# A two-layer decoder trunk on one core: the down projections take the operands in two halves over four open column tiles

## The chip, the core and the metric

The kernel runs on one core of a Trainium2 chip. Five engines work side by side on that core, each in the order of its own instruction stream, and wait for each other by semaphores: TensorE (PE in the profile) multiplies matrices into PSUM, VectorE (DVE) and ScalarE (ACT) work element by element and may read PSUM, GpSimd (POOL) works element by element in SBUF, and SyncE (SP) issues the transfers from and to the device's memory. The metric is the time of one execution in microseconds (us) of device time; lower is better.

## The reference

The reference is two decoder layers over 256 tokens of width 1024. Each layer ends in a feed-forward block, and the change lies in that block alone:

```python
def conv_ffn(x, norm_g, w_up, conv_w, conv_b, w_down):
    s_ = x.shape[1]
    u = rmsnorm(x, norm_g) @ w_up
    up = jnp.pad(u, ((0, 0), (CONV_W - 1, 0), (0, 0)))
    c = conv_b + up[:, 0:s_] * conv_w[0]
    for j in range(1, CONV_W):
        c = c + up[:, j:j + s_] * conv_w[j]
    val, gate = jnp.split(c, 2, axis=-1)
    return (jax.nn.silu(gate) * val) @ w_down
...
    for l in range(DEPTH):          # DEPTH = 2: an mLSTM layer, then an attention layer
        h = h + (mixer of layer l)(h)
        h = h + conv_ffn(h, f_norm[l], f_w_up[l], f_conv_w[l], f_conv_b[l], f_w_down[l])
```

`w_up` is 1024 by 5632 (value and gate halves of 2816), `w_down` is 2816 by 1024, all in float32.

## The kernel before

The residual stream is kept transposed, as eight tiles of 128 features by 256 tokens (`hT`). Every float32 operand is split exactly into a high and a low part, and a product is three passes of parts. One call of `one(k)` in `steps_w`, called a step here, is two matmuls into one PSUM tile: the low weights by the high operand (256 columns, line 245) and the high weights by both parts of the operand side by side (512 columns, line 241). For k = 0 the order of the two is the other way round.

**The feed-forward block.** The up projection has 22 pairs, value and gate of 128 features each, in two PSUM tiles per pair. `finish` takes a pair out of PSUM (`whole`, lines 281 and 282), runs the three-tap convolution (lines 326 and 329), the gate (line 336) and the product (line 338), and splits the result into the high part (line 339, on ACT) and the low part (line 340, on POOL) of one of the 22 operands `f0` to `f21` of the down projection.

**The down projection.** It has eight column tiles, n = 0 to 7, of 128 features; each sums 22 steps, one for each operand. `down(n, ks)` gives the steps of tile n for the operands in ks. In the kernel before they go in this order: tile 0 with operands 0 to 18, tile 1 with 0 to 10, tile 0 with 19 to 21, tile 1 with 11 to 21, then tiles 2 to 7 whole. After a tile's last step, `residual` adds it to `hT` (lines 289 and 291); in layer 0 `feed` then makes the next stage's two sets of operands (lines 180 and 181), in layer 1 the tile is written out (line 293).

`project_out`, which the two mixers use for their output projections, already takes its operands in two halves over four column tiles (`GROUP = 4`), with eight steps to a tile.

**Weights.** `w_down` is held in 16 units per layer, two for each column tile: unit 2n has operands 0 to 10 of tile n, unit 2n + 1 has 11 to 21. A unit is loaded by one transfer of 704 KB on the SP queue into one of three `raw` buffers, and split in two pieces by ACT (line 171, the high part) and DVE (line 172, the low part) into one of four `hi` and four `lo` buffers. A unit is made when its first step is emitted, so the order of the steps is the order of the units too.

**What sets the order.** PE runs in the order of the program text. DVE, ACT, POOL and SP run in an order that a scheduler fixes at build time. Sums of this kind lie in a pool of five PSUM tiles, `pacc`, used in turn.

Of the kernel before, what the change touches and what calls it, by code (L numbers as in the profile page):

```python
# [20 lines left out]
S = 256  # L21
KD = D // P
NT = S // P
FF = 2816
KF = FF // P
# [4 lines left out]
DH = 128  # L30
# [6 lines left out]
AHEAD = 2  # L37
GROUP = 4
WARM = 8
WHOLE = 6  # L40
PIECES = 2

# columns of the per-partition parameter array
C_KVNORM, C_BNORM, C_FNORM, C_HN = 0, 8, 16, 32
# [3 lines left out]
N_PAR = C_CB + L * 2 * KF  # L48
# columns of the array that is needed first: the gates' weights, the first gain
C_WG, C_ANORM = 0, KD * 2 * MH  # L50
# [5 lines left out]
class Once:  # L56
    """A thing that is made when it is first asked for."""

# [9 lines left out]
def mix(steps, items=()):  # L68
    """Emit the steps, each a (cost, function), and the items, each a (time, function), among them."""
    items, now = list(items), 0.0  # L70
    for cost, step in steps:
        while items and items[0][0] <= now:
            items.pop(0)[1]()
        step()
        now += cost
    for _, item in items:
        item()
# [3 lines left out]
def yoco_kernel(ctx: ExitStack, tc: tile.TileContext, A, out):  # L81
    nc = tc.nc
    # the tensor engine works in the order of this program
    ctx.enter_context(tc.manual_schedule(engines={mybir.EngineType.PE}))
# [8 lines left out]

    # ---- the residual stream, transposed: hT[:, k] holds features k*128.. by tokens
    hT = keep.tile([P, KD, S], F32, name="hT")
    fst = const.tile([P, N_FIRST], F32, name="fst")
    par = const.tile([P, N_PAR], F32, name="par")
    # rows on every partition: the gates' biases, the gains of k's and q's first 32 features
    row = const.tile([P, N_ROW], F32, name="row")
# [17 lines left out]

    # the gates' weights: for each k the high parts, the low parts, and zeros
    wgs = wsp.tile([P, 2048], F32R, name="hi")[:, :KD * P]
    mhalf = const.tile([P, 8], F32, name="mhalf")  # L120
    nc.gpsimd.memset(mhalf, -0.5)
    # while the first loads run: the tensor engine's clock rises, the activation tables are loaded
    nc.scalar.activation(const.tile([P, 1], F32, name="tables"), mhalf[:, :1], AF.Exp)
    warm = const.tile([P, 512], BF16, name="warm")
    nc.vector.memset(warm, 0.0)
    for j in range(WARM):
# [3 lines left out]

    # ---- constants made on the chip
    ident = const.tile([P, P], F32, name="ident")
    make_identity(nc, ident)
    # adds rows m and m + 8
    both8 = const.tile([4 * MH, 2 * MH], F32, name="both8")
    nc.gpsimd.tensor_tensor(out=both8, in0=ident[:4 * MH, :2 * MH], in1=ident[:4 * MH, 2 * MH:4 * MH], op=OP.add)
    # sel[:, h] has ones in row h alone
    sel = const.tile([MH, MH, P], F32, name="sel")
    nc.gpsimd.memset(sel, 0.0)
    nc.gpsimd.affine_select(out=sel, in_=sel, pattern=[[-1, MH], [0, P]],  # L140
                            compare_op=OP.not_equal, fill=1.0, base=0, channel_multiplier=1)
    # [s, t], 1 where s <= t, else 0; columns 128.. are ones
    tri = const.tile([P, S], F32, name="tri")
    nc.gpsimd.memset(tri, 1.0)
    nc.gpsimd.affine_select(out=tri[:, :P], in_=tri[:, :P], pattern=[[1, P]],
                            compare_op=OP.is_ge, fill=0.0, base=0, channel_multiplier=-1)
    # mLSTM: [s, t], 0 where s <= t, else BIG; columns 128.. are free
    cmask = const.tile([P, S], F32, name="cmask")
# [4 lines left out]
    nc.gpsimd.tensor_copy(identb, ident)  # L153
    # attention: [t, s], columns 128.. 0 where s <= t, else -BIG; the columns before are free
    amaskf = const.tile([P, S], F32, name="amaskf")
# [5 lines left out]

    # ---- weights: a unit is loaded whole and split exactly into two float32r parts
    def unit(src, length, raw=None, pieces=PIECES):
# [18 lines left out]

    # ---- RMSNorm: the gain goes into the matmul's operand, 1/rms is applied to its result
    # an operand: for each k its high part, its low part, and both side by side
    def operand(pool, name, n):
# [20 lines left out]
    class Rstd:  # L206
        """1/rms of the residual stream: a column over the tokens and a row on every partition."""

# [15 lines left out]

    # ---- matmuls: three exact passes of hi and lo parts
    def steps_w(ps, w, at, x, ks, kall, done=None, apart=True):
        """ps[n, tokens] += W[k, n].T x[k, tokens]; at(k) gives the columns of k in w. The high parts of W
        times the low parts of x may be summed apart, in the second half of ps."""
        xh, xl, both = x
# [23 lines left out]
    def steps_x(t, units, x, done):  # L253
        """ps[tokens, 512] = x[k, tokens].T W[k, 512] over two units of four k."""
        xh, xl, _ = x
# [14 lines left out]
    def block_x(src, first, x, done):  # L270
        """Both token tiles of 512 columns: units first and first + 1 of src."""
        u = [Once(lambda j=j: unit(src[first + j], 2048)) for j in range(2)]
        return [s for t in range(NT) for s in steps_x(t, u, x, done)]
# [4 lines left out]
    def whole(ps, rows=P):  # L278
        """Both halves of a result of steps_w, in SBUF."""
        y = work.tile([P, S], F32, name="whole", bufs=WHOLE)[:rows]  # L280
        nc.scalar.activation(y, ps[:rows, S:], AF.Copy)  # L281
        nc.vector.tensor_tensor(y, ps[:rows, :S], y, OP.add)  # L282
        return y
# [13 lines left out]
    def project_out(src, x, gains, items):  # L297
        """GROUP columns' tiles go on with each operand as it comes, the items among their first half."""
        w = [Once(lambda u=u: unit(src[u], 2048)) for u in range(4)]
# [10 lines left out]

    # ---- ConvFFN
    def conv_ffn(l, gains):
        r = Rstd()
        with tc.tile_pool(name=f"ffn{l}", bufs=1, reuse_waits="tile") as fp, \
# [27 lines left out]
            def rescale():  # L342
                # the operands once more, with 1/rms in them
                r.row()
# [14 lines left out]
            ps = [[Once(acc) for half in range(2)] for i in range(KF)]  # L359
            # the first pairs go on with each operand as it comes  # L360
            mix([s for k in range(KD) for i in range(AHEAD) for s in pair_k(pair, i, k)],
# [15 lines left out]

            mix(down(0, range(19)) + down(1, range(11)) + down(0, range(19, KF)) + down(1, range(11, KF)))
            for n in range(2, KD):
                mix(down(n, range(KF)))  # L380
# [3 lines left out]

    # ---- layer 0: the first operands
    wgv = wgs.rearrange("p (k m) -> p k m", k=KD)
# [12 lines left out]
    with tc.tile_pool(name="mls", bufs=1, reuse_waits="tile") as mp, \  # L399
            tc.tile_pool(name="mlw", bufs=2, reuse_waits="tile") as mw:  # L400
        r = Rstd()
        # gates: parts of the input gates, then of the forget gates, by tokens
        psg = acc()
# [60 lines left out]
        def decay(h):  # L464
            # transposed: E[s, t] = exp(a_s - M_t), 0 where s > t
            mb = mis()[:, :S]
# [8 lines left out]

        # k and q by head, features by tokens
        kq = [mp.tile([P, S], F32, name=f"kq{j}") for j in range(2 * MH)]
# [15 lines left out]

        # the gates and the first unit go on with each operand as it comes
        def gate_step(k):
# [11 lines left out]

        # S^T times the decay weights
        PT = [[mp.tile([P, 384], F32R, name=f"PT{h}{j}") for j in range(2)] for h in range(MH)]
# [10 lines left out]

        # v with a column of ones and one of zeros: high parts, low parts
        V = [[mp.tile([P, MH, MV + 2], F32R, name=f"V{t}{j}") for j in range(2)] for t in range(NT)]
# [13 lines left out]

        # numerators and denominators, tokens by features
        hs = {}
# [24 lines left out]

        # output gates
        def o_done(nb):
# [18 lines left out]
        def at(t0, dt, fn, args):  # L584
            return [(t0 + dt * i, lambda a=a: fn(*a)) for i, a in enumerate(args)]
# [9 lines left out]

    # the rotation's tables with the gains of k and q in them; the other features' gains as columns
    tab = const.tile([P, 2, NT, 2, ROT], F32, name="tab")
# [13 lines left out]

    # ---- layer 1: attention over one block of 256 tokens
    with tc.tile_pool(name="att", bufs=1, reuse_waits="tile") as mp, \
# [4 lines left out]
        ys = {}  # L618
        # a query's factors: DH^-0.5 / rms, by head
        cq = mp.tile([P, NT, 2, 4], F32, name="cq")  # L620
        ncq = mp.tile([P, NT, 2, 4], F32, name="ncq")

        def heads(i, nb):
            def done(t, ps):
# [14 lines left out]
                if i == 0:  # L639
                    c = factor()  # L640
                    nc.vector.tensor_tensor(y, y, c[:, :, None].to_broadcast([P, 4, DH]), OP.mult)
                # rotate the first 32 features of each head
                r1 = mw.tile([P, 4, 2, HALF], F32, name="r1")
# [83 lines left out]
def _cols(w):  # L727
    """[k, n] -> units of 256 columns: [unit, 128, 8 * 256]."""
    k, n = w.shape
    return w.reshape(k // P, P, n // 256, 256).transpose(2, 1, 0, 3).reshape(n // 256, P, -1)  # L730


def _rows(w):
    """[k, n] -> units of 512 rows by 512 columns: [column block * 2 + row half, 128, 4 * 512]."""
    k, n = w.shape
    return w.reshape(2, 4, P, n // 512, 512).transpose(3, 0, 2, 1, 4).reshape(n // 256, P, 2048)
# [57 lines left out]
```

## Time and profile before

| | us |
|---|---|
| median of 3 runs | 608.62 (608.0 to 608.84) |
| span of the profiled execution, first to last instruction | 607.1 |
| PE busy | 593.5 (98% of the span) |
| DVE busy | 495.6 (82%) |
| ACT busy | 393.2 (65%) |
| POOL busy | 171.8 (28%) |

For the profiled execution the profile gives the span alone. A run's time also holds what lies ahead of the first and behind the last instruction; the median of the runs is 1.5 us above this span. Busy PE is modelled from the starts of its matmuls, so small gaps between matmuls count as busy.

### The profile page before, as it was taken

The numbers are of one execution on the slowest core, as the hardware profiler recorded it, in microseconds if no ns is written. First come the engines' busy times: TensorE is split into PE (matmuls) and PEld (weight loads), VectorE is DVE, ScalarE is ACT, GpSimd is POOL, SyncE is SP. The second block draws the span as 40 slices with busy tenths as digits, with TensorE's granted clock in tenths as the row PEclk, the third lists the DMA queues.
The fourth block names the chain that finished last, engine by engine and source line by source line (L and its number), as shares of the span: only waits on it lengthen the run. The fifth ranks groups of instructions, "written<-read, shape, count | busy, mean of one in ns | idle before, by whom it ended". The sixth has DMA issues, their size and how long they took to land.

```text
span 607.1 us, 8990 instructions
## 1 busy us (share of the span) xinstructions
PE 593.5 (98%) x3278; PEld 505.9 (83%) x3278; DVE 495.6 (82%) x837; ACT 393.2 (65%) x713; POOL 171.8 (28%) x186
## 2 busy tenths in 40 slices
PE   7899999999999999899999999999999999998997
PEld 4787888888888888788888878888888888887887
DVE  7897667989999999967768786467999999998550
ACT  5756776667886777755556687554878767675330
POOL 6600310352545344211111100022445453441000
PEclk8999999999999999899999999999999999999999
DMA  6874333526444543465754533335353445336530
GB/s 243 317 264 169 139 138 140 208 84 263 159 179 166 191 165 133 161 207 184 266 203 181 198 123 143 125 135 208 132 215 140 185 172 198 138 131 229 212 108 18
DMA packets 18621, 105.79 MB, mean 174 GB/s; under 512 B 2320, under 2 KB 3856, under 8 KB 9104
## 3 DMA queue, kind: packets, MB, share of 16 engines
q1 hardware_dynamic: 18576, 105.21, 47.0%
q8 instruction: 26, 0.43, 0.3%
q14 instruction: 19, 0.16, 0.1%
HBM read 104.15 MB, written 1.05 MB: 173 GB/s over the span
## 4 chain that ended last, share of the span: by engine, by line
PE 48%; DVE 37%; issue 8%; ACT 3%; POOL 2%; DMA 1%; SPq 0%; POOLq 0%; DVEq 0%; ACTq 0%
PE acc L241 15%; DVE y L329 15%; DVE lo L172 14%; PE acc L245 8%; PE acc L262 6%; PE acc L264 6%; PE acc L263 6%; DVE whole L282 4%; DVE xs L348 1%; ACT y L326 1%; DVE xa L181 1%; PE acc L239 1%; ACT hi L171 1%; DMA hT<-xT 1%; PE mis L547 1%
## 5 line engine op out<-in xcount | busy, mean ns | idle before, releaser
L172 DVE TENSOR_TENSOR lo<-raw,hi 128x1024 fp32r<-128x1024 f32 (+2 forms) x218 | 248.6, 1168 | 30.5 <-ACT hi L171 30.2
L241 PE MATMUL acc<-xb,hi 128*128 128x512 f32 x736 | 252.3, 396 | 0.6 <-POOL xb L351 0.6
L171 ACT ACTIVATE hi<-raw 128x1024 fp32r<-128x1024 f32 (+2 forms) x218 | 199.9, 964 | 61.3 <-PE acc L241 29.5
L245 PE MATMUL acc<-xb,lo 128*128 128x256 f32 x736 | 191.2, 279 | 0.0
L241 PEld LDWEIGHTS acc<-xb,hi 128*128 128x128 f32 x736 | 131.8, 188 | 26.3 <-POOL xb L351 1.3
L245 PEld LDWEIGHTS acc<-xb,lo 128*128 128x128 f32 x736 | 138.7, 188 | 8.0
L241 PE MATMUL acc<-f,hi 128*128 128x512 f32 x330 | 116.6, 398 | 1.0 <-POOL f L340 1.0
L329 DVE SCALAR_TENSOR_TENSOR y<-whole,par,y 128x254 f32<-128x254 f32 (+1 forms) x176 | 110.0, 644 | 3.2 <-ACT y L326 2.8
L245 PE MATMUL acc<-f,lo 128*128 128x256 f32 x352 | 97.5, 284 | 3.0 <-ACT f L339 3.0
L338 POOL TENSOR_TENSOR a<-sg,y 128x256 f32<-128x256 f32 x44 | 57.8, 1314 | 98.4 <-ACT sg L336 98.4
L241 PEld LDWEIGHTS acc<-f,hi 128*128 128x128 f32 x330 | 61.8, 190 | 14.5 <-POOL f L340 1.4
L245 PEld LDWEIGHTS acc<-f,lo 128*128 128x128 f32 x352 | 66.8, 190 | 5.0 <-ACT f L339 3.6
L326 ACT ACTIVATE y<-whole,par 128x256 f32<-128x256 f32 x88 | 51.7, 594 | 20.8 <-DVE whole L282 18.8
L241 PE MATMUL acc<-xa,hi 128*128 128x512 f32 x160 | 57.5, 401 | 0.7 <-DVE hT L291 0.5
L262 PE MATMUL acc<-hi,xa 128*128 128x512 f32 x128 | 53.4, 417 | 0.0
L340 POOL TENSOR_TENSOR f<-a,f 128x256 fp32r<-128x256 f32 x44 | 42.3, 962 | 36.6 <-ACT f L339 36.6
L264 PE MATMUL acc<-hi,xa 128*128 128x512 f32 x128 | 50.1, 391 | 0.0
L199 POOL TENSOR_TENSOR sqacc<-sqacc,sq 128x256 f32<-128x256 f32 x18 | 16.3, 908 | 119.0 <-ACT sq L198 119.0
L263 PE MATMUL acc<-lo,xa 128*128 128x512 f32 x128 | 50.0, 391 | 0.0
L245 PE MATMUL acc<-xa,lo 128*128 128x256 f32 x160 | 44.4, 289 | 0.8 <-DVE lo L172 0.7
L282 DVE TENSOR_TENSOR whole<-acc,whole 128x256 f32<-128x256 f32 (+1 forms) x97 | 39.4, 412 | 0.0
L281 ACT ACTIVATE whole<-acc 128x256 f32<-128x256 f32 (+1 forms) x97 | 35.4, 368 | 6.0 <-PE acc L241 5.8
(180 smaller groups left out, 637.7 us busy)
## 6 DMA issues: line engine op xcount, KB each, us to landing
raw<-w_up SPq DMA_DIRECT2D x44, 1024.0 KB, 4.8
raw<-w_down SPq DMA_DIRECT2D x32, 704.0 KB, 4.0
raw<-w_kqv SPq DMA_DIRECT2D x12, 1024.0 KB, 4.8
raw<-w_vo SPq DMA_DIRECT2D x8, 1024.0 KB, 4.8
raw<-w_out SPq DMA_DIRECT2D x4, 1024.0 KB, 4.8
raw<-w_o SPq DMA_DIRECT2D x4, 1024.0 KB, 4.8
raw<-w_kq SPq DMA_DIRECT2D x2, 1024.0 KB, 7.8
raw<-w_kq SPq DMA_DIRECT2D x4, 256.0 KB, 5.5
```

The costliest lines, as they stand in the source:

```text
L171: nc.scalar.activation(hi[:, c], raw[:, c], AF.Copy)
L172: nc.vector.tensor_tensor(lo[:, c], raw[:, c], hi[:, c].bitcast(F32), OP.subtract)
L241: nc.tensor.matmul(p, hi[:, c], both[k], start=k == 0, stop=last)
L245: nc.tensor.matmul(p[:, :S], lo[:, c], xh[k], start=False, stop=False)
L262: nc.tensor.matmul(p, xh[k][:, ts], hi[:, c], start=k == 0, stop=False)
L263: nc.tensor.matmul(p, xh[k][:, ts], lo[:, c], start=False, stop=False)
L264: nc.tensor.matmul(p, xl[k][:, ts], hi[:, c], start=False, stop=k == KD - 1)
L282: nc.vector.tensor_tensor(y, ps[:rows, :S], y, OP.add)
L326: nc.scalar.activation(y, u, AF.Identity, bias=b, scale=w[2])
L329: nc.vector.scalar_tensor_tensor(y[:, d:], u[:, :S - d], w[j], y[:, d:], op0=OP.mult, op1=OP.add)
L338: nc.gpsimd.tensor_tensor(out=a, in0=sg, in1=y[0], op=OP.mult)
L340: nc.gpsimd.tensor_tensor(out=al[i], in0=a, in1=ah[i].bitcast(F32), op=OP.subtract)
```

## The change

A constant `HOLD = 4` is new, and the last lines of `conv_ffn` emit the steps in another order. Comments are taken out elsewhere, and all lines below the constant move down by one, so that line 241 of before is line 242 after. The number of matmuls, weight units, transfers and vector operations is the same.

```diff
+HOLD = 4
...
-            mix(down(0, range(19)) + down(1, range(11)) + down(0, range(19, KF)) + down(1, range(11, KF)))
-            for n in range(2, KD):
+            for ks in (range(KF // 2), range(KF // 2, KF)):
+                for n in range(HOLD):
+                    mix(down(n, ks))
+            for n in range(HOLD, KD):
                 mix(down(n, range(KF)))
```

On PE, layer 0, where tile 0 (`acc_2683`) meets the last operands, 30 steps after the projection's first, the kernel before has these rows (a name is the PSUM tile, then the operand and the part of the weights, each with its buffer's number; `f18_1257` is operand 18):

```order
L241 MATMUL acc_2738<-f10_1249,hi_2732 128x512
L245 MATMUL acc_2683<-f19_1258,lo_2709 128x256
L241 MATMUL acc_2683<-f19_1258,hi_2708 128x512
L245 MATMUL acc_2683<-f20_1259,lo_2709 128x256
L241 MATMUL acc_2683<-f20_1259,hi_2708 128x512
L245 MATMUL acc_2683<-f21_1260,lo_2709 128x256
L241 MATMUL acc_2683<-f21_1260,hi_2708 128x512
L245 MATMUL acc_2738<-f11_1250,lo_2777 128x256
```

Tile 0 returns for operands 19 to 21 right after the first half of tile 1 (`acc_2738`). In the changed kernel the same place, the end of tile 0, stands 22 steps later on PE, and these rows are the change to the second half and the end:

```order
L242 MATMUL acc_2776<-f10_1249,hi_2770 128x512
L246 MATMUL acc_2683<-f11_1250,lo_2802 128x256
L242 MATMUL acc_2683<-f11_1250,hi_2801 128x512
...
L246 MATMUL acc_2683<-f21_1260,lo_2802 128x256
L242 MATMUL acc_2683<-f21_1260,hi_2801 128x512
L246 MATMUL acc_2714<-f11_1250,lo_2839 128x256
```

Four tiles (`acc_2683`, `acc_2714`, `acc_2745`, `acc_2776`) have taken operands 0 to 10 before any takes operand 11, so operand 11 is first read after 44 steps and operand 21 after 54.

On DVE, layer 0, behind the convolution of the last pair (`y`), the kernel before has these rows (`lo` is the low part of a weight unit, `hT` with `acc` the residual's sum):

```order
L172 TENSOR_TENSOR lo_2777<-raw_2774,hi_2776 128x704 x2
L329 SCALAR_TENSOR_TENSOR y_2665<-whole_2662,par_80,y_2665 128x255
L329 SCALAR_TENSOR_TENSOR y_2665<-whole_2662,par_80,y_2665 128x254
L172 TENSOR_TENSOR lo_2816<-raw_2813,hi_2815 128x704 x2
L172 TENSOR_TENSOR lo_2847<-raw_2844,hi_2846 128x704
L289 TENSOR_TENSOR hT_78<-acc_2683,hT_78 128x256
L172 TENSOR_TENSOR lo_2847<-raw_2844,hi_2846 128x704
L291 TENSOR_TENSOR hT_78<-acc_2683,hT_78 128x256
```

In the changed kernel the same stretch of DVE reads:

```order
L173 TENSOR_TENSOR lo_2771<-raw_2768,hi_2770 128x704 x2
L330 SCALAR_TENSOR_TENSOR y_2665<-whole_2662,par_80,y_2665 128x255
L330 SCALAR_TENSOR_TENSOR y_2665<-whole_2662,par_80,y_2665 128x254
L173 TENSOR_TENSOR lo_2802<-raw_2799,hi_2801 128x704 x2
L173 TENSOR_TENSOR lo_2839<-raw_2836,hi_2838 128x704 x2
L173 TENSOR_TENSOR lo_2878<-raw_2875,hi_2877 128x704 x2
L173 TENSOR_TENSOR lo_2917<-raw_2914,hi_2916 128x704 x2
L290 TENSOR_TENSOR hT_78<-acc_2683,hT_78 128x256
L292 TENSOR_TENSOR hT_78<-acc_2683,hT_78 128x256
```

Up to the last `y` the kinds of rows are the same in both, and only which unit a split belongs to differs. Behind it, four whole units are split ahead of the first residual sum, where it was one and a half. Layer 1 differs in the same way. On SP, eleven loads of `w_down` in layer 1 stand ahead of the first output, where it was nine; POOL's order is the same in both.

## Rows read from the trace of the kernel before

**Rows 1.** The page, its 40 slices: the clock that TensorE was granted, in tenths.

```profile
PEclk8999999999999999899999999999999999999999
```

**Rows 2.** Busy us by stretch: PE, PEld, DVE, ACT, POOL; granted clock; DMA share; GB/s.

```profile
250.00:260.00 10.00, 8.19 (x38) 6.67 (x36) 8.78 (x13) 5.99 (x11) 1.75 (x3) 0.83 0.65 224
260.00:270.00 10.00, 10.00 (x59) 8.77 (x58) 6.76 (x12) 5.98 (x11) 0.86 (x1) 1.00 0.58 206
...
550.00:560.00 10.00, 7.83 (x44) 6.45 (x43) 8.81 (x13) 5.15 (x8) 1.61 (x2) 1.00 0.84 288
```

**Rows 3.** Who waited for whom, PE, 200 to 320 us: total, times, longest.

```profile
PE acc L245 <- ACT f L339: 1.3, 1, 1.3
PE acc L241 <- POOL f L340: 0.5, 1, 0.5
```

**Rows 4.** The same view of PE, 490 us to the end.

```profile
PE acc L245 <- ACT f L339: 1.7, 1, 1.7
...
```

**Rows 5.** Timeline of PE, layer 0: start, duration, what, idle before in brackets.

```profile
251.65 0.39 PE L241 MATMUL acc<-f,hi 128*128 128x512 f32 x1
...
252.00 0.39 PE L241 MATMUL acc<-f,hi 128*128 128x512 f32 x1
253.70 0.39 PE L245 MATMUL acc<-f,lo 128*128 128x256 f32 x1 [1.31 <-ACT f L339]
254.59 0.80 PE L241 MATMUL acc<-f,hi 128*128 128x512 f32 x1 [0.50 <-POOL f L340]
...
257.91 0.40 PE L241 MATMUL acc<-f,hi 128*128 128x512 f32 x1
```

**Rows 6.** Timeline of PE, layer 1.

```profile
550.04 0.39 PE L241 MATMUL acc<-f,hi 128*128 128x512 f32 x1
...
552.98 0.50 PE L241 MATMUL acc<-f,hi 128*128 128x512 f32 x1 [0.51 <-POOL f L340]
...
553.78 0.40 PE L241 MATMUL acc<-f,hi 128*128 128x512 f32 x1
```

**Rows 7.** Two equal stretches behind layer 0's wait, columns as in rows 2.

```profile
255.00:257.90 2.90, 2.90 (x10) 2.41 (x10) 2.76 (x6) 2.36 (x6) 0.00 (x0) 0.51 0.81 270
257.90:260.80 2.90, 2.90 (x19) 2.56 (x18) 1.84 (x4) 0.70 (x3) 0.00 (x0) 1.00 0.88 303
```

**Rows 8.** The matmuls of one tile name, by window: duration min/median/max, first and last start.

```profile
L241 PE MATMUL acc<-f,hi x32: 387/394/400, 241.0 to 252.0; 128*128 128x512 f32 x32
...
L241 PE MATMUL acc<-f,hi x32: 387/395/400, 539.1 to 550.0; 128*128 128x512 f32 x32
```

**Rows 9.** Timeline of DVE, layer 0.

```profile
243.42 2.22 DVE L172 TENSOR_TENSOR lo<-raw,hi 128x704 fp32r<-128x704 f32 x2
...
248.34 0.41 DVE L282 TENSOR_TENSOR whole<-acc,whole 128x256 f32<-128x256 f32 x1
248.68 2.22 DVE L172 TENSOR_TENSOR lo<-raw,hi 128x704 fp32r<-128x704 f32 x2
250.82 0.99 DVE L329 SCALAR_TENSOR_TENSOR y<-whole,par,y 128x255 f32<-128x255 f32 x2
251.73 2.22 DVE L172 TENSOR_TENSOR lo<-raw,hi 128x704 fp32r<-128x704 f32 x2
```

**Rows 10.** The instructions on one tile name: duration min/median/max in ns, first, last.

```profile
L289 DVE TENSOR_TENSOR hT<-acc,hT x32: 409/425/425, 101.0 to 603.8; 128x256 f32<-128x256 f32 x32
...
L181 DVE SCALAR_TENSOR_TENSOR xa<-hT,par,xa x24: 469/478/960, 102.7 to 419.4; 128x256 fp32r<-128x256 f32 x24
```

**Rows 11.** The page, transfers: count, KB each, us from issue to landing.

```profile
raw<-w_down SPq DMA_DIRECT2D x32, 704.0 KB, 4.0
```

**Rows 12.** Busy us in the attention's output projection (w_o), columns as in rows 2.

```profile
390.00:412.00 22.00, 22.00 (x136) 19.53 (x136) 16.10 (x27) 13.01 (x23) 3.57 (x4) 1.00 0.48 175
```

## The prediction

> **What bounds the kernel now.** I read the page's slices first, then the stretches of the two down projections, then PE's waits and its timeline there. The slices show TensorE at its full clock everywhere but at the start and in the 17th slice [rows 1], which lies in layer 0's down projection. By stretches, PE is busy 8.19 of 10 us at 250 to 260, with a mean granted clock of 0.83, and 7.83 of 10 at 550 to 560 in layer 1, at full clock; ten us later in layer 0 it is at 10.00 of 10 [rows 2]. So PE bounds both projections, but for a hole in each. The list of PE's waits says what the holes are: in 120 us around layer 0's projection there are two entries, both for an `f` operand of that projection, its high part from ACT (line 339) and its low part from POOL (line 340) [rows 3], and in layer 1 the same two [rows 4, 6]. The timeline gives the place: PE takes operand 20 at 252.00, waits for operand 21 until 254.59, and then goes slowly until 257.91 [rows 5]. DVE explains why operand 21 is late: the convolution of the last pair, at 250.82, stands behind a weight unit's split at 248.68, and the next split follows it at 251.73 [rows 9].
>
> **The change, step by step.** It removes no work. It moves operand 21's first use from step 32 of the projection (19 + 11 steps, then operands 19, 20, 21) to step 54 (four tiles with 11 steps each, then operands 11 to 21).
>
> *What the holes cost.* Steps start every 0.35 us (251.65 and 252.00 [rows 5]). From 252.00 to 257.91 PE makes six steps, which at that pace take 2.10 us and took 5.91: 3.81 us lost. Of it, 2.24 us is the wait (254.59 - 252.00 - 0.35), and 1.57 us is the slow stretch behind it (five steps in 3.32 us, against 1.75). That the slow stretch is the clock is seen in two equal stretches of 2.9 us: 10 matmuls at a granted 0.51, then 19 at 1.00 [rows 7], so the lower of the two levels, 1.2 GHz, came after a wait of 2 us with one matmul in it. In layer 1 there are three steps from 550.04 to 553.78 [rows 6]: 3.74 - 1.05 = 2.69 us lost, all of it wait, since the clock stays at 1.00 [rows 2]. Together 6.50 us.
>
> *Does operand 21 come in time after?* The projection's first step is at 241.0 [rows 8], so step s starts at about 241.0 + 0.35 s. Operand 21 is complete when PE goes on at 254.59 [rows 5] and is wanted at 241.0 + 54 x 0.35 = 259.9: 5.3 us early. In layer 1 the projection starts at 539.1 [rows 8], and the operand is there at 552.98 [rows 6] for a step at 558.0: 5.0 us early. DVE's order up to the last `y` is the same as before, so the operand is made no later than it was.
>
> *Do the weights come in time?* Units are used in the order 0, 2, 4, 6, 1, 3, 5, 7, each for 11 steps (3.85 us), so the same number per microsecond as before. The third is split on DVE by 245.6 (243.42 + 2.22) and wanted at step 22, 248.7. The fourth is split from 248.68 to 250.9 [rows 9]; its first half, there at about 249.8, is wanted at step 33, 252.6: 2.8 us early. The fifth (251.73 [rows 9], first half at about 252.8) is wanted at step 44, 256.4: 3.6 us early. Layer 1 has the tightest of them: its projection starts 298.1 us after layer 0's [rows 8] and the unit comes in the same rhythm, so I take 2 us as the least margin. From the fifth on DVE goes through four units without the residual's sums between them, 8.9 us by 2.22 each, and PE uses a unit in 3.85 us, so the splits stay ahead. The four `hi` and `lo` buffers help: a unit is now given back every 3.85 us, while before, unit 1 was held from step 11 to the end of the wait.
>
> *Do the PSUM tiles come in time?* Four held tiles and the next one are all five of `pacc`. Each takes the place of a pair's tile, in the order in which the pairs are taken out. The last of these reads is at 248.34 to 248.75 [rows 9], and its place goes to tile 4, wanted at step 88, 271.8. Tile 3, wanted at 252.6, takes the place before it, which was read earlier still.
>
> *What moves behind.* Tile 0 is done at step 55 instead of 33, tile 1 at 66 instead of 44, tile 2 at 77 instead of 66, tile 3 at 88 as before. So the first four residual sums come every 3.85 us. Each brings DVE two sums and two operand parts in layer 0, 2 x 0.43 + 2 x 0.48 [rows 10], besides a unit's split: 4.0 us with the 2.22 of rows 9, a little over 3.85. Three such rounds leave DVE about half a microsecond late, and the weights are units ahead by then. Tiles 4 to 7 are as before, and DVE was busy 6.76 of 10 us there [rows 2]. On SP, loads and outputs change places in layer 1: the 12th load of `w_down` waits for the first output, due at 539.1 + 55 x 0.35 = 558.4 and some 0.9 us of sums; with 4.0 us to land [rows 11] and 2.2 to split it is there by 566, for step 121, 581.5. All this I cost at nothing.
>
> *Sum.* 607.1 - 6.5 = 600.6 us of span. The runs' median is 1.5 us above the span profiled, which gives 602.1. The loss in the profiled execution need not be the median run's: the clock fell behind one of two like waits, so a run before may have had none, one or two such falls, at 1.57 each. If the median run had two, the time outside the span is nearly nothing and the changed kernel is at 608.62 - 8.07 = 600.5; if it had none, at 608.62 - 4.93 = 603.7.
>
> **The rivals.**
>
> *The clock falls elsewhere.* The waits go, but one stretch at the lower level turns up in the projection or a later stage: 602.1 + 1.6 = 603.7. For it: the two waits were alike, and one brought a fall and one none, so what starts one is not read from the wait's length alone. Against it: apart from the start and behind that wait, no slice has less than 9 tenths [rows 1], and no other wait of PE is in these stretches [rows 3, 4].
>
> *Another wait takes the place.* PE stops at tile 3 for the fourth unit, the tightest of the margins above. That needs DVE to be over 2 us later than in rows 9, and then costs what is beyond 2 us; DVE's order and its inputs up to there are those of before. If half of the old wait came back in each layer, with no slow stretch: 602.1 + 2.4 = 604.5.
>
> *Nothing is gained.* If DVE, and not PE, set the pace through the projections, taking PE's hole away would only let PE wait at the next unit: 608.6. Against it: behind 260 DVE is busy 6.76 of 10 us and PE 10.00 [rows 2].
>
> *Slower.* Changing the PSUM tile might leave TensorE idle for moments, and each such moment might drop the clock. The change makes seven changes of tile among the held four where there were three, in two layers eight more. At 1.57 us for each fall: 602.1 + 8 x 1.57 = 614.7, and five falls are enough to eat the gain (6.5 / 1.57 = 4.1). Against it: the output projection of the attention steps through four held tiles in the same way, and has 22.00 of 22.00 us busy at a clock of 1.00 [rows 12]. The Trainium skill (TensorE: Matmul & The Clock Gate, A second HAM failure mode: psum-queue depth-cycling) describes this: a kernel that cycles through PSUM banks lets the engine idle briefly and often between groups of matmuls, and its clock swings between the two levels. By that rule the time would be this rival's; the stretch at 390 to 412 does not show it.
>
> **How the numbers follow.** A change within 0.2%, 1.2 us, can't be told from none here. The forecast, both waits gone and nothing in their place, has 0.80. The clock falling elsewhere has 0.08, part of the wait coming back 0.06, nothing gained 0.03, slower by the clock 0.03. The first three lie below 607.4, so faster has 0.94, same 0.03, slower 0.03. The range goes from the lower bound of the time outside the span, less the few tenths by which runs differ (600.5 - 0.3), to its upper bound with one fall of the clock (603.7 + 1.6): 600.2 to 605.3.
>
> **What the new profile would show.** PE's waits for `f` from lines 340 and 341 are gone from both projections; the slices are at 9 throughout behind the start; the stretch 250 to 260 has PE at 10.00 and the clock at 1.00. The first residual sum of layer 0's projection is near 260.5 instead of 255.4, and everything behind layer 0 is 3.8 us earlier, the end 6.5. I am wrong if PE waits for `lo` at the start of tile 2 or 3, if the clock is below 1 in either projection, or if PE waits at the start of the attention for operands that the bunched sums delay.

## The result, and the profile after

The changed kernel takes 602.35 us (602.21 to 602.65, 4 runs) against 608.73 us (608.0 to 610.46, 4 runs) of the kernel before on the same chip: a ratio of 0.9891, 95% interval 0.9875 to 0.9906. That is 6.4 us less, where 602.1 us, 6.5 us less, was forecast.

The page of the changed kernel gives this span, and this clock over the 40 slices. Against [rows 1] the 8 in the 17th slice is gone:

```profile
span 600.5 us, 8992 instructions
...
PEclk8999999999999999999999999999999999999999
```

Busy time by stretch of the changed kernel, columns as in [rows 2]; the two stretches that held the holes are full and at full clock, and DVE's busier time has moved to 260 to 270, where the first residual sums now come together:

```profile
250.00:260.00 10.00, 10.00 (x59) 8.78 (x58) 7.89 (x11) 6.05 (x10) 1.62 (x2) 1.00 0.70 216
260.00:270.00 10.00, 10.00 (x58) 8.74 (x58) 9.05 (x17) 7.17 (x14) 0.86 (x1) 1.00 0.76 257
...
550.00:560.00 10.00, 10.00 (x59) 8.79 (x58) 7.26 (x12) 4.99 (x7) 0.00 (x0) 1.00 0.89 279
```

The list of PE's waits, from 200 to 320 us and from 490 us to the end, has no entry at all, where [rows 3] and [rows 4] had the two for `f`. Why it is empty is seen on GpSimd and on TensorE. First GpSimd's last row for operand 21 in layer 0, then PE's last row for operand 20 and its first for operand 21, then where the attention's first projection begins:

```profile
253.53 0.82 POOL L341 TENSOR_TENSOR f<-a,f 128x256 fp32r<-128x256 f32 x1 [0.53 <-ACT f L340]
```

```profile
259.48 0.40 PE L242 MATMUL acc<-f,hi 128*128 128x512 f32 x1
259.71 0.28 PE L246 MATMUL acc<-f,lo 128*128 128x256 f32 x1
...
302.54 0.39 PE L263 MATMUL acc<-hi,xa 128*128 128x512 f32 x1
```

The operand is complete at 253.53 + 0.82 = 254.35, within 0.25 us of where it was before [rows 5], and PE reads it at 259.71, 5.4 us later. The attention begins 3.9 us earlier than in the kernel before, whose row is this; so much of the saving is made by then:

```profile
306.47 0.40 PE L262 MATMUL acc<-hi,xa 128*128 128x512 f32 x1
```

DVE of the changed kernel from the fourth unit's split to the first residual sum, to set beside [rows 9]:

```profile
248.46 2.23 DVE L173 TENSOR_TENSOR lo<-raw,hi 128x704 fp32r<-128x704 f32 x2
250.62 0.99 DVE L330 SCALAR_TENSOR_TENSOR y<-whole,par,y 128x255 f32<-128x255 f32 x2
251.53 2.23 DVE L173 TENSOR_TENSOR lo<-raw,hi 128x704 fp32r<-128x704 f32 x2
254.17 3.33 DVE L173 TENSOR_TENSOR lo<-raw,hi 128x704 fp32r<-128x704 f32 x4 [0.42 <-ACT hi L172]
259.16 1.69 DVE L173 TENSOR_TENSOR lo<-raw,hi 128x704 fp32r<-128x704 f32 x2 [1.65 <-ACT hi L172]
260.77 0.42 DVE L290 TENSOR_TENSOR hT<-acc,hT 128x256 f32<-128x256 f32 x1
```

Up to 253.76 DVE does what it did before, at the same pace. Then it splits three units with idle time between them, and the eighth unit is ready at 260.85 for a step at 240.8 + 77 x 0.35 = 267.8. The fourth unit was the tightest, as forecast: its first half was split by about 249.6 (248.46 and half of 2.23), for step 33 at 240.8 + 33 x 0.35 = 252.4, 2.8 us early. In layer 1 the same unit's split starts at 542.81, so its first half was there at about 543.9 for a step at 546.8, 2.8 us early as well.

### The profile page after: what moved, and what is told of

Same layout as the page of the kernel before. It is cut to its first block, busy times and chain, and to the rows that moved or that the text cites. A ratio compares the mean times of both kernels' runs of the same rounds, so it can differ in the third digit from the quotient of the medians.

```text
span 600.5 us, 8992 instructions
## 1 busy us (share of the span) xinstructions
PE 591.0 (98%) x3278; PEld 504.8 (84%) x3278; DVE 495.4 (82%) x837; ACT 393.0 (65%) x713; POOL 172.7 (29%) x186
## 4 chain that ended last, share of the span: by engine, by line
PE 87%; DVE 6%; ACT 3%; POOL 2%; issue 1%; DMA 1%; SPq 0%; DVEq 0%; POOLq 0%
PE acc L242 41%; PE acc L246 21%; PE acc L263 6%; PE acc L265 6%; PE acc L264 6%; DVE lo L173 3%; ACT hi L172 1%; DVE xs L349 1%; DVE xa L182 1%; PE acc L240 1%; DMA hT<-xT 1%; PE mis L551 1%; POOL tab L611 1%; DVE hT L292 1%; PE mis L666 1%
## 5 line engine op out<-in xcount | busy, mean ns | idle before, releaser
L242 PE MATMUL acc<-f,hi 128*128 128x512 f32 x330 | 115.0, 394 | 0.0
## 6 DMA issues: line engine op xcount, KB each, us to landing
raw<-w_kq SPq DMA_DIRECT2D x4, 256.0 KB, 5.4
```

Source lines behind the costliest of these rows:

```text
L242: nc.tensor.matmul(p, hi[:, c], both[k], start=k == 0, stop=last)
```

## The experiments

Nine kernels were run, in three sets, each beside the kernel before on its chip (608.84 to 608.97 us in the median). Each is the changed kernel with one edit, but for one that has operand 21 late in the old order: there the last lines of `conv_ffn` are those of before as well.

**Two tiles held, in halves.** Operand 21 falls back to step 32, and every weight unit is still used in one piece:

```diff
-HOLD = 4
+HOLD = 2
```

> Two tiles are held open instead of four, again in halves of eleven operands. Operand 21 is then first wanted at step 32 (11 + 11 + 10), the same step as in the kernel before, while every weight unit is used in one piece, as in the changed kernel. My theory (what counts is the step at which operand 21 is first wanted): both waits are back, 608.6 us, 608.0 to 610.5. Rival (the gain is from the units, each given back after 11 steps, or from the plain halves): 602.4, as with four.

Measured: 609.04 us (607.87 to 611.6), ratio 1.0004 (0.9989 to 1.0019). The whole gain is gone. PE's waits in layer 0:

```profile
PE acc L246 <- ACT f L340: 1.8, 1, 1.8
PE acc L242 <- POOL f L341: 0.5, 1, 0.5
```

The same two waits of [rows 3] are back in both layers, so neither the halves nor the units' order gain anything by themselves while operand 21 is wanted at step 32.

**Three tiles held.** Operand 21 is wanted at step 43:

```diff
-HOLD = 4
+HOLD = 3
```

> Three tiles are held open. Operand 21 is wanted at step 43: 241.0 + 43 x 0.35 = 256.1 in layer 0, and it is there at 254.5; 539.1 + 15.1 = 554.2 in layer 1, there at 553.0. My theory: both waits are gone with 1.2 to 1.6 us to spare, and the time is that of four tiles, 602.4 (602.0 to 603.0). Rival (four open tiles are needed, the gain goes by the number of tiles): between the two kernels, 604 to 607.

Measured: 602.4 us (602.29 to 603.17), ratio 0.9892 (0.9869 to 0.9914), as with four. In its trace operand 21 is complete at 254.44 and the projection starts at 240.9, so step 43 is at 256.0: 1.5 us to spare are as good as 5.4.

**Two tiles held, nineteen operands each.** Operand 21 is wanted at step 40:

```diff
-            for ks in (range(KF // 2), range(KF // 2, KF)):
-                for n in range(HOLD):
+            for ks in (range(19), range(19, KF)):
+                for n in range(2):
                     mix(down(n, ks))
-            for n in range(HOLD, KD):
+            for n in range(2, KD):
```

> Only two tiles are held, but each takes 19 operands before it stops: tile 0 with 0 to 18, tile 1 with 0 to 18, then 19 to 21 of either. Operand 21 is wanted at step 40, 255.0 in layer 0 (there at 254.5) and 553.1 in layer 1 (there at 553.0). My theory: the waits are gone or a few tenths of a us each, 602.4 to 603.0. Rival (halves, or more than two open tiles, are what gains): 607 to 609.

Measured: 602.31 us in the median (602.27 to 606.58), ratio 0.9887 (0.9862 to 0.9913); the run of 606.58, the profiled one, has some ten us at the lower clock between 20 and 35 us, before either projection. This is one of these stretches; the changed kernel has 30 matmuls there at a clock of 1.00:

```profile
25.00:30.00 5.00, 5.00 (x18) 4.15 (x17) 3.19 (x7) 0.97 (x3) 0.00 (x0) 0.50 0.46 187
```

PE has no wait in either projection here. Operand 21 is complete at 258.86 for a step at 245.3 + 40 x 0.35 = 259.3 in layer 0 (all of it later by the slow stretch), and at 553.11 for 553.5 in layer 1: 0.4 us to spare were enough. Two tiles suffice when they keep PE busy until step 40. With two tiles in halves, which end in the waits, this says that the step of operand 21 counts, not the number of tiles.

**One layer at a time.** For layer 0 (and the same with 1):

```diff
+            if l == 0:
+                for ks in (range(KF // 2), range(KF // 2, KF)):
+                    for n in range(HOLD):
+                        mix(down(n, ks))
+            else:
+                mix(down(0, range(19)) + down(1, range(11)) + down(0, range(19, KF)) + down(1, range(11, KF)))
+                for n in range(2, HOLD):
+                    mix(down(n, range(KF)))
             for n in range(HOLD, KD):
```

> The new order in layer 0 alone, the old one in layer 1. My theory: the two waits are independent; layer 1's stays, at 2.7 us, 602.4 + 2.7 = 605.1, or 606.6 if the clock falls behind it in this run. Rival (nearly all the gain is in one layer, or a saving in layer 0 only lets layer 1 wait longer): 602.4 or 608.7.

> The new order in layer 1 alone, the old one in layer 0. My theory: layer 0's wait stays, at 2.2 us without and 3.8 us with the slow stretch behind it: 604.6 to 606.2. Rival: 602.4 or 608.7, as for layer 0 alone. The two gains, 608.7 less this time and 608.7 less that of layer 0 alone, should add up to the 6.4 us of the whole change within 1.6, one fall of the clock.

Measured: 604.66 us for layer 0 alone (604.55 to 604.94), ratio 0.9928 (0.9906 to 0.995); 606.46 us for layer 1 alone, ratio 0.9953 (0.9937 to 0.997). The second is 0.3 us above the range expected. Against the 608.92 us of before in this set that is 4.26 us and 2.46 us, together 6.7, where both give 6.4 to 6.6. So the two holes are independent, to within 0.3 us. Of the ten runs of layer 1 alone two are at 604.65 and 604.76, six from 606.02 to 606.78 and two near 607.5. The profiled run is the one of 604.76, and in its trace layer 0's wait is there and the clock does not fall behind it, while in [rows 2] the same wait has 0.83:

```profile
250.00:260.00 10.00, 8.17 (x46) 6.72 (x45) 9.20 (x15) 7.00 (x13) 1.72 (x3) 1.00 0.71 226
```

So the wait itself costs 604.7 - 602.35 = 2.35 us. The six runs above it by 1.3 to 2.1 us fit a slow stretch like the 1.57 us of [rows 5], but only the run of 604.76 has a trace, so where they lost it is not shown.

**Tiles in turn.** Tiles 4 and 5 step by step:

```diff
-            for n in range(HOLD, KD):
+            mix([s for k in range(KF) for n in (4, 5) for s in down(n, [k])])
+            for n in range(6, KD):
                 mix(down(n, range(KF)))
```

> The changed kernel, with tiles 4 and 5 of both layers taken in turn, one step of each: 43 changes of the PSUM tile per layer where there was one. My theory: a change of tile costs TensorE nothing, 602.4 (602.0 to 603.5), and the granted clock stays at 1.00 in that stretch. Rival (changes of tile leave idle moments and bring the clock down): 1.6 us for each fall, and a clock below 1 around 272 to 288 us; five falls make it 610.

Measured: 602.36 us (602.31 to 603.17), ratio 0.9888 (0.9867 to 0.991). The stretch with the 43 changes, as busy time, and three matmuls in it, the last of one step and the two of the next, which goes into the other tile:

```profile
272.00:288.00 16.00, 16.00 (x94) 14.00 (x92) 8.02 (x14) 6.22 (x11) 0.79 (x1) 1.00 0.53 183
```

```profile
273.03 0.39 PE L242 MATMUL acc<-f,hi 128*128 128x512 f32 x1
273.26 0.28 PE L246 MATMUL acc<-f,lo 128*128 128x256 f32 x1
273.38 0.40 PE L242 MATMUL acc<-f,hi 128*128 128x512 f32 x1
```

Steps start 0.35 us apart as within one tile, and the clock stays at 1.00. The rival that ended slower is refuted for tiles whose operands are there.

**Operand 21 made late.** Multiplications by one on GpSimd, in place, behind the last pair's product; four of them in the new order, four in the old order, eight in the new:

```diff
                 nc.gpsimd.tensor_tensor(out=a, in0=sg, in1=y[0], op=OP.mult)
+                for _ in range(4 if i == KF - 1 else 0):
+                    nc.gpsimd.tensor_tensor(out=a, in0=a, in1=tri[:, P:P + 1].to_broadcast([P, S]), op=OP.mult)
```

> The changed kernel, with operand 21 made late: four more multiplications by one, in place, one after the other on GpSimd, behind its product. By the product's own 0.8 to 1.3 us they take 3.2 to 5.2 us. My theory: operand 21 has 5.3 us to spare in layer 0 and 5.0 in layer 1, so nothing or at most a few tenths are lost: 602.4 to 603. Rival (the operand is not what PE waited for, or the spare time is smaller): up to 5.2 us per layer, 606 to 613.

> The same lateness in the old order, where PE already waits for operand 21. My theory: each of the two waits grows by all of the 3.2 to 5.2 us, and the clock falls behind both: 608.7 + 6.4 + 1.6 = 616.7 at the least, 620.7 at the most. Rival (PE's wait had another cause that ends at the same time): 608.7 to 612.

> The changed kernel, with operand 21 made twice as late: eight extra multiplications on GpSimd instead of four. With four, PE's wait for operand 21 in the old order grew from 1.3 to 4.6 us in each layer, 3.3 us, so eight make it 6.6 us late. My theory: the spare time is 5.3 us in layer 0 and 5.0 in layer 1, so PE waits again, 1.3 and 1.6 us plus 0.5 for the low part: 602.4 + 3.9 = 606.3; ACT stands still meanwhile, so the sixth weight unit may be late as well, which would add up to 2 us in each layer, and a fall of the clock 1.6: 605.5 to 611. Rival (the spare time is larger, or PE does not wait for this operand): 602.4 to 603.2, as with four.

Measured with four: 603.16 us in the new order (602.41 to 603.7), ratio 0.9897 (0.9875 to 0.9919); 618.11 us in the old (616.41 to 618.88), ratio 1.0138 (1.0105 to 1.0171). The same edit costs 9.3 us in one order and 0.8 in the other, by the medians. GpSimd in the new order, layer 0, the four extra rows and the low part of operand 21:

```profile
253.27 4.28 POOL L341 TENSOR_TENSOR a<-a,tri 128x256 f32<-128x256 f32 x4
258.08 0.74 POOL L343 TENSOR_TENSOR f<-a,f 128x256 fp32r<-128x256 f32 x1 [0.53 <-ACT f L342]
```

It is complete at 258.82, before the 259.9 at which it is wanted, and PE has no wait in this run, which took 602.41 us; the other three took 603.12 to 603.7, so that the median is 0.2 above the range expected, and why is not shown. PE in the old order, layer 0:

```profile
253.00 0.39 PE L242 MATMUL acc<-f,hi 128*128 128x512 f32 x1
258.02 0.58 PE L246 MATMUL acc<-f,lo 128*128 128x256 f32 x1 [4.62 <-ACT f L342]
258.83 0.80 PE L242 MATMUL acc<-f,hi 128*128 128x512 f32 x1 [0.23 <-POOL f L343]
```

The wait is 258.83 - 253.00 - 0.35 = 5.5 us instead of 2.2, 3.2 us longer; in layer 1 it grows from 2.6 to 5.45, by 2.9. The slow stretch in layer 0 costs 2.3 us instead of 1.57, and layer 1, which [rows 6] show without one, has one of 1.5. That is 8.3 of the 9.3 us. The last one is not the operand's: this run begins layer 0's projection at 242.04 instead of 241.0, and its clock is at 0.66 from 20 to 25 us, where the kernel before has 1.00.

Measured with eight in the new order: 609.35 us (608.0 to 611.03), ratio 1.0006 (0.9985 to 1.0028). The eight took 8.10 us on GpSimd, more than the 6.6 that I took for them from the old order, where the operations are shorter (four in 3.21 us). PE in layer 0:

```profile
259.51 0.40 PE L242 MATMUL acc<-f,hi 128*128 128x512 f32 x1
261.73 0.39 PE L246 MATMUL acc<-f,lo 128*128 128x256 f32 x1 [1.81 <-ACT f L342]
262.53 0.79 PE L242 MATMUL acc<-f,hi 128*128 128x512 f32 x1 [0.42 <-POOL f L343]
```

The waits are back: 262.53 - 259.51 - 0.35 = 2.7 us at step 54 in layer 0, and as much in layer 1. That is the lateness less the spare time, 8.1 - 5.4 = 2.7. With the slow stretch behind the first, 1.4 us, it makes 602.35 + 2 x 2.7 + 1.4 = 609.15, and this run took 609.05. So what the change bought is this spare time: it would be used up by an operand some 5.4 us later.

## Why the prediction was right, point by point

**The holes were the whole gain, and both closed.** 607.1 - 600.5 = 6.6 us of span against 6.50 worked out from [rows 5] and [rows 6]. The empty list of waits and the slices show it; holding two tiles in halves brings both waits back, with the halves and the order of the units still in place, and takes the whole gain away.

**Operand 21 in time.** Forecast 5.3 us early in layer 0 and 5.0 in layer 1; measured 5.4 in layer 0 (254.35 for 259.71) and 5.4 in layer 1 (548.69 for 535.2 + 54 x 0.35 = 554.1). Four extra operations used most of it without a wait, eight went past it.

**Weights, PSUM, residual sums: cost nothing.** No wait of PE in either projection names a weight or a tile. The first sum came at 260.77, forecast near 260.5. The bunched sums show as DVE's 9.05 us of 10 at 260 to 270, and PE did not wait for them. What was mis-stated in this step is only the claim that DVE would split four units in a row at 2.22 us: it waited for ACT in between (0.42 and 1.65 us idle), and the pieces of the last three units were shorter, 0.83 to 0.85 us each.

**The time outside the span.** It was taken as 1.5 us, with 0 to 3.1 as bounds. The changed kernel's profiled execution took 602.21 us with a span of 600.5, 1.7 us outside; so did that of two tiles in halves (611.6 and 609.9). So the profiled execution of before, 607.1 + 1.7 = 608.8, was near the median, with one fall of the clock behind the two waits, and the bounds were wider than needed.

**The terms by layer.** Layer 1's hole was sized at 2.69 us and is worth 604.66 - 602.35 = 2.3 alone; layer 0's was sized at 3.81 and is worth 606.46 - 602.35 = 4.1 in the median. The sum holds better than its parts, and that is luck: one term was 0.4 us too large and the other 0.3 too small, since one execution's waits stood for those of the median run and the two misses nearly cancel. In layer 1 of the execution in [rows 6] PE stood idle for the operand's high part for 1.67 us, in the profiled run with layer 0 changed for 1.33.

**The rivals.** Another wait in its place and no gain are excluded by the empty list of waits. The slower rival, and with it the Trainium skill's account (TensorE: Matmul & The Clock Gate, A second HAM failure mode: psum-queue depth-cycling), had its test in the tiles taken in turn: 43 changes of tile per layer at a clock of 1.00 and no time lost. That section's case has idle moments between the groups; here there are none, since each group's operands and weights are there, so the rule is not refuted for its own case. It doesn't apply to changes of tile as such.

That rival was also sized wrongly. The order of before, tiles 0, 1, 0, 1, 2, 3, has five changes among the four tiles and not three, so the new order adds four changes in two layers and not eight. Priced as there, that is 602.1 + 4 x 1.57 = 608.4 and not 614.7, no slower than before.

The clock falling elsewhere was not seen in the changed kernel's profiled run, but it happens to kernels of either order, near the start: at 20 to 35 us with nineteen operands each, which cost that run 4.3 us, and at 20 to 25 us with two tiles in halves (0.68) and in the old order with operand 21 late (0.66). The change lies behind these stretches and does nothing against them.

## What to carry to other kernels

When the engine that bounds a kernel waits for the last of a row of operands, count the steps between the start and the first use of that operand, and compare with when it is complete: open accumulators are a way to have other work in those steps, and 0.4 us of spare time were as good as five. The number of open tiles is not the aim; two that go on long enough did as well as four. Check the margins of what the new order asks for earlier (weights, free tiles) from the timeline, and find the real margin by making the operand late on purpose.

## What the runs showed of the hardware

A wait of the same length brings TensorE's clock down in some executions and not in others. In the profiled ones, waits of 2.2 us (layer 0 of before), 2.3 and 2.7 us (both layers with two tiles in halves), 2.7 us (layer 0 with eight late operations) were followed by a stretch at the lower level; waits of 2.6 us (layer 1 of before), 2.3 and 2.3 us (one layer at a time) and 2.7 us (layer 1 with eight) were not. The waits of 5.5 us, in both layers, were. What decides among the short ones stays open. Their length does not: a fall came behind 2.2 and 2.3 us, and none behind two others of 2.3 and one of 2.6. In the traces a fall behind a short wait costs 1.4 to 1.7 us, behind a wait of 5.5 us 1.5 to 2.3. The kernel before varies from 607.1 to 612.4 us over 21 runs of one set, the changed one by 0.4 over its four; the falls behind the waits can make a part of that, and those near the start another, but only one run of each kernel has a trace.

On GpSimd the same multiplication took 0.80 us in the old order, where DVE stood idle but for the first 0.7 us, and 1.07 us in the new, where DVE was splitting weights for the first 3.1 us (four in 3.21 us and in 4.28 us; single ones lie between 0.61 and 1.14). DVE's pieces took 1.17 us beside them (four in 4.68 us), against 0.83 in the changed kernel, so each was slower while the other worked. This was not expected, and why they differ wasn't tried.

Single runs of 603.2 us among 602.3 us (three tiles, tiles in turn) are unexplained too, and so are the 0.8 us by which the median with four late operations lies above. With tiles in turn and with four late operations the slower runs have a mean granted clock of 0.994 to 0.997 and the others 0.999 to 1.000, which fits a fall of the clock somewhere; with three tiles 0.997 stands at 603.17 and at 602.34 alike.
